# Column pairs for a short down projection, two scratch pools, an earlier norm chain, and three recurrent tiles projected ahead

## The chip, the core and the metric

The kernel runs on one core of a Trainium2 chip. The metric is device time in microseconds (us) of one execution. Engines are named as the profile names them: PE is TensorE's matmul (PEld its weight loads), ACT is ScalarE, DVE is VectorE, POOL is GpSimd, SP is SyncE, whose queue issues nearly all loads.

## The reference

Two residual layers over 256 tokens of width 2048. Layer 0 mixes tokens by attention, layer 1 by a gated linear recurrence; each is followed by a SwiGLU block of hidden width 5632. In short:

```python
for i in range(2):
    h = rms_norm(x, norm_mix[i])
    x = x + (attention_mixer(h, ...) if i == 0 else recurrent_mixer(h, ...))
    h = rms_norm(x, norm_ffn[i])
    x = x + (silu(h @ w_gate[i]) * (h @ w_up[i])) @ w_down[i]

# recurrent_mixer
xb, yb = split(h @ w_in, 2)
xb = depthwise_conv_width_4(xb) + bias
r, i = sigmoid(block_diag(xb, w_a) + b_a), sigmoid(block_diag(xb, w_i) + b_i)
log_a = -8 * r * softplus(-lam);  u = sqrt(1 - exp(2 * log_a)) * i * xb
h_t = exp(log_a_t) * h_(t-1) + u_t        # once forward, once backward in time
out = ((h_fwd + h_bwd) * gelu(yb)) @ w_out
```

Everything is in float32.

## The kernel before

**Products.** Each float32 operand is split into a rounded high part and a low rest (`hi`, `lo`), and a product is three matmuls: high by high, high by low, low by high. Weights arrive as halves of 8 blocks of 128x128 (512 KB, `load_half`, L110): a load on SP into `raw`, a cast on ACT to `hi` (L123), a subtraction on DVE to `lo` (L124), with five buffers of each. The list `order` (L163 to L171) fixes the sequence of all the halves.

**PE's order is written by hand**, instruction by instruction in program order. A counter, `step()`, advances once per triple of matmuls in the recurrence; `later(delay, fn)` hangs small work (the norm's broadcast, gates, scans) on a later step. The other engines' orders come from a planner that simulates the program; each engine then runs its list in order.

**FFN.** The hidden width is cut into parts of 12, 16 and 16 contraction tiles (`PARTS`). A part is made in units of four hidden tiles: gate and up projections as a pair of 512-wide columns (`unit`, `project_pair`), then `turned` (L458) transposes the product to feature-major (`tb`, then 16 copies into `tf`), and L795 and L796 split it into the operands `act`. Then the part is projected down and added to the residual `x_tok`. In a pair, two of the eight contraction steps (`SEVEN`, steps 2 and 5) use seven products in place of eight: `seven_forms` makes three sums of weights (`wx`, `wxh`, `wxl`, L264 to L272), `x_forms` the matching sums of operands, and `merge` (L333 to L337) puts the banks together. A step of a pair is two loads: 24 matmuls of 512 columns, or 21 with seven products. `down` does this for the 16-tile parts; the 12-tile part goes through `output` (L490), one column after another over all of its tiles, its matmuls at L247.

**Norm.** `Norm.add(c)` follows each finished column of the residual: squares with their sums, `turned`, then four operands `xg` (L418, L419). After the last column `finish()` makes the inverse root mean square, and for the recurrence's norm `spread()` makes diagonal matrices `ndg` (L444); 26 steps later two pairs of small matmuls (L450) turn them into a row vector per token, `nr.r` (`nrb`, L452).

**Recurrence.** It has 16 x tiles and 16 y tiles, in 8 blocks of two x and two y tiles. A tile is 16 contraction steps of three 256-wide matmuls (L341 to L343). Before block 0, `project_two` projects x tiles 0 and 1 over contraction tiles 0 to 11, then both over 12 to 15. The iteration of block b projects the x tiles of block b + 1 and the y tiles of block b, and has the gates, decays, scans and finishing of block b hung on the steps in `WHEN`. `conv_branch` (L822) multiplies a tile by `nr.r` into `cb`, convolves it in PSUM into `xc` and splits it into `xs`, the gates' operand. `load_gates` (L848) loads `graw`, casts it on ACT (`ghi`, L856) and subtracts on POOL (`glo`, L857).

**Scratch.** The FFN's scratch (`tb`, `tf`, `wx`, `fg`, `fu` and more) is one pool, `fp`. It is closed after layer 0, and the recurrence's pool `rp` is opened on the same memory; a tile there waits until what lay in its place was last read. PSUM has four banks for long sums (`acc`) and four for the rest (`pm`).

Of the kernel before, what the change touches and what calls it, by code (L numbers as in the profile page):

```python
# [31 lines left out]
LAST_STEPS = (0, 1, 3, 2, 4, 5, 6, 7)  # L32
# [4 lines left out]
COMMON = {"nsq", "nr", "nrt", "rsq_s", "nj", "ndg", "nrb"}  # L37
EPS = 1e-6
# [5 lines left out]
NORM = 26  # L44
# [7 lines left out]
WHEN = (18, 25, 32, 39, 42, 46, 50, 54, 58, 60, 62, 64, 66, 70, 74)  # L52
WHEN_LAST = (5, 9, 13, 17, 19, 20, 21, 24, 24, 25, 26, 27, 33, 39, 39)
# [20 lines left out]
def trunk(ctx, tc, w, out):  # L74
# [64 lines left out]
    def unit_steps(first):  # L139
        return FIRST_STEPS if first else USUAL_STEPS, True  # L140

    def down_steps(p, second):
        last = p == len(PARTS) - 1
        return LAST_STEPS if second and last else USUAL_STEPS, True

    def ffn_order(l):
        units = [wide(f"w_gate{l}"), wide(f"w_up{l}")]
        seq, i = [], 0
        for p, n in enumerate(PARTS):
            for _ in range(n // FOUR):  # L150
                for k, cols in pair_plan(*unit_steps(i == 0)):
# [105 lines left out]
    def seven_forms():  # L257
        load_half(*order[taken[0]])
        r1, w1 = flat(newest["raw"]), [flat(t) for t in newest["tiles"]]
        x, xh, xl = (fp[0].tile([P, 3, WIDE], t, tag=n, name=nm(n), bufs=1) for n, t in (("wx", F32), ("wxh", F32R), ("wxl", F32R)))  # L260
# [11 lines left out]
        dve.tensor_tensor(xl, x, xh[:].bitcast(F32), ALU.subtract)  # L272
        taken[0] += 2
        return [[t[:, k, :] for t in w] for w, k in ((w1, 0), (w1, 1), (w2, 0), (w2, 1), ((xh, xl), 0), ((xh, xl), 1), ((xh, xl), 2))]

    def x_forms(h0, h1, tag):
# [6 lines left out]
        t = fp[0].tile([P, 2, 4, P], F32R, tag=tag, name=nm(tag), bufs=1)  # L283
# [4 lines left out]
    def project_pair(xs, forms, order, middle, done):  # L288
        banks = [[new_acc() for _ in range(2)] for _ in range(2)]
        begun = set()  # L290

# [10 lines left out]
        steps = pair_plan(*order)  # L302
        seven = [n for n in order[0] if n in forms]
        for n, cols in steps:
            if n in forms:
# [6 lines left out]
                product(banks[0][0], tokens(2 * n + 1, 0), b21)  # L312
                product(banks[1][0], s4, b22)
# [3 lines left out]
                product(banks[0][1], tokens(2 * n + 1, 1), t4)  # L317
                if last:
                    middle(p1, q5, q6, q7)
            else:  # L320
                for j in cols:
                    half()
                    hi, lo = (flat(t) for t in newest["tiles"])
                    end = n == order[0][-1]
                    for a in range(2):
                        for k in range(2):
                            product(banks[j][a], tokens(2 * n + k, a), (hi[:, k, :], lo[:, k, :]), end and k == 1)
                    if end:
                        done(j, banks[j])

    def merge(p1, q5, q6, q7):
        g, u = (fp[0].tile([P, 2, WIDE], F32, tag=t, name=nm(t), bufs=1) for t in ("fg", "fu"))
# [72 lines left out]
    class Norm:  # L405
# [28 lines left out]
        def finish(self):  # L434
# [3 lines left out]
            self.rt = rsqrt(ms, "nr")  # L438


        def spread(self):
            dg = tmp("ndg", bufs=1)
            for a in range(2):
                dve.tensor_scalar(dg[:, a * P : (a + 1) * P], ident, self.rt[:, a : a + 1], None, ALU.mult)  # L444
# [8 lines left out]

            later(NORM, stage)

    def turned(src, both=True):  # L458
# [4 lines left out]
        for q in range(4):  # L463
            for i in range(4):
                o, y = f[32 * i : 32 * i + 32, q::4, :, :], b[32 * q : 32 * q + 32, :, i, :]
                y = y.rearrange("p a (k t) -> p a k t", k=FOUR)
                if i % 2 and both:
                    dve.tensor_copy(o, y)
                else:
                    act.copy(o, y)  # L470
# [4 lines left out]
    def open_ffn():  # L475
        fp[:] = [ffn_scope.enter_context(tc.tile_pool(name=nm("fp"), bufs=1))]
# [13 lines left out]
    def output(xs, norm=None, end=False, ready=0, close=None):  # L490
# [12 lines left out]
        if norm is not None:  # L503
            norm.finish()


    def down(xs, forms, p, norm=None, end=False):
        for c in (0, 2):
# [19 lines left out]
            project_pair(xs, forms, down_steps(p, c > 0), middle, done)  # L528
        if norm is not None:
            norm.finish()  # L530
# [244 lines left out]
    def ffn(norm, nxt):  # L775
        def unit(hid, forms, first):
# [12 lines left out]
            project_pair(norm.xs, norm.forms, unit_steps(first), lambda *banks: got.extend(merge(*banks)), done)  # L789
# [8 lines left out]
            for i, n in enumerate(SEVEN):  # L798
                if forms is not None and first <= 2 * n < len(hid):
                    forms[n] = x_forms(hid[2 * n], hid[2 * n + 1], f"hf{i}")  # L800

        for p, n in enumerate(PARTS):
            hid, forms = [], {} if n == KT else None
            for i in range(n // FOUR):
                unit(hid, forms, p == i == 0)
# [3 lines left out]
            if n == KT:  # L809
                down(hid, forms, p, nxt if last else None, last and nxt is None)  # L810
            else:
                output(hid)
# [4 lines left out]
    nr.spread()  # L817
# [3 lines left out]
    scope.append(rt.enter_context(tc.tile_pool(name="rp", bufs=2)))  # L821
# [99 lines left out]
    for b in range(-1, NBLK):  # L921
        blk, nxt = nxt, Block(b + 1) if b + 1 < NBLK else None
        if blk:
# [16 lines left out]
    def end_recurrence():  # L940
        rt.close()
        scope.pop()
# [91 lines left out]
```

## Time and profile before

| | |
|---|---|
| median of 3 runs | 2022.96 us (2022.78 to 2024.07) |
| the profiled execution's own time | 2022.37 us |
| its span, first to last instruction | 2020.6 us |
| PE busy | 1995.2 us, 99% of the span |
| DVE, ACT busy | 1666.0 us (82%), 1320.7 us (65%) |
| matmuls | 9944 |
| HBM read | 382.13 MB, 190 GB/s over the span |

Stages by the line of the matmuls, from the span's start: attention with its projections to 268 us (its output projection's columns from 184 on), layer 0's first part of the FFN to 395.6, its down projection to 467.5, the other two parts to 977.0, the recurrence to 1222.2, its output projection to 1309.5, layer 1's FFN to the end.

A profile row names line, engine, operation, the tile written and those read. "Busy" is the time in instructions; a matmul's end is modelled, so that matmuls overlap in the rows, and their starts tell the pace. "Granted clock" is the share of TensorE's full clock in a window. An idle time in brackets stands before an instruction, with the instruction that ended it.

### The profile page before, as it was taken

To read this page: it belongs to the slowest core of one execution; us is meant where nothing else is said; L and a number is where in the kernel's file an instruction comes from. 1 tells how busy PE (TensorE), PEld (TensorE's weight loads), DVE (VectorE), ACT (ScalarE), POOL (GpSimd) and SP (SyncE) were. 2 spreads that over 40 slices of the span, in tenths; PEclk is the share of its full clock that TensorE was granted. 3 is DMA by queue.
4 is the path that set the end of the run, shared out by engine and by line. 5 is a ranking of instruction groups with operands and counts; after the bars stand their busy time and mean duration, and the time that the engine had idled before them with its cause. 6 is when DMAs were issued, how large, how long until landed. Compare 5 with 4: busy or idle time off the path is not lost.

```text
span 2020.6 us, 27860 instructions
## 1 busy us (share of the span) xinstructions
PE 1995.2 (99%) x9944; PEld 1696.2 (84%) x9944; DVE 1666.0 (82%) x2347; ACT 1320.7 (65%) x2054; POOL 165.7 (8%) x213
## 2 busy tenths in 40 slices
PE   9999999999999999999899999999999999999999
PEld 8898888878888888887799998888788888888887
DVE  8998788856888888889868887898657898878897
ACT  7666666644667546677688898667545766457663
POOL 1463000000000000000133330000000000000000
PEclk9999999999999999999999999999999999999999
DMA  8444665656555665555555555655566566665564
GB/s 320 158 137 140 193 200 187 207 168 198 192 195 187 219 208 188 190 195 192 188 163 188 178 179 174 200 188 187 195 185 202 185 204 206 203 192 187 196 222 146
DMA packets 109004, 386.06 MB, mean 191 GB/s; under 512 B 12225, under 2 KB 12993, under 8 KB 108737
## 3 DMA queue, kind: packets, MB, share of 16 engines
q1 hardware_dynamic: 108720, 384.26, 58.0%
q8 instruction: 78, 1.28, 0.3%
q14 instruction: 62, 0.50, 0.1%
q10 hardware_dynamic: 144, 0.02, 0.0%
HBM read 382.13 MB, written 2.10 MB: 190 GB/s over the span
## 4 chain that ended last, share of the span: by engine, by line
PE 52%; issue 41%; DVE 4%; DMA 1%; ACT 1%; POOL 0%; DVEq 0%; SPq 0%; ACTq 0%; POOLq 0%
PE acc L294 24%; PE acc L247 7%; PE acc L225 6%; PE pm L294 4%; PE acc L341 3%; PE acc L342 3%; PE acc L343 3%; DVE lo L124 2%; PE pm L342 1%; PE pm L343 1%; PE pm L341 1%; DMA raw<-in_w_up_dram 1%; ACT hi L123 0%; DMA graw<-in_w_gates_dram 0%; ACT tf L470 0%
## 5 line engine op out<-in xcount | busy, mean ns | idle before, releaser
L123 ACT CAST hi<-raw 128x1024 fp32r<-128x1024 f32 (+1 forms) x708 | 730.4, 1045 | 486.1 <-PE acc L294 314.1
L124 DVE TENSOR_TENSOR lo<-raw,hi 128x1024 fp32r<-128x1024 f32 (+1 forms) x708 | 857.4, 1228 | 172.0 <-ACT hi L123 169.9
L294 PE MATMUL acc<-hi,xg 128*128 128x512 f32 x2200 | 694.4, 389 | 2.3 <-DVE fg L783 1.2
L294 PEld LDWEIGHTS acc<-hi,xg 128*128 128x128 f32 x2200 | 412.9, 188 | 91.0 <-DVE fg L783 2.0
L294 PE MATMUL acc<-lo,xg 128*128 128x512 f32 x1100 | 427.9, 389 | 0.0
L247 PE MATMUL acc<-hi,act 128*128 128x512 f32 x896 | 283.4, 395 | 6.2 <-ACT act L795 5.4
L294 PE MATMUL acc<-hi,act 128*128 128x512 f32 x800 | 252.7, 389 | 0.0
L294 PEld LDWEIGHTS acc<-lo,xg 128*128 128x128 f32 x1100 | 206.5, 188 | 42.4
L247 PEld LDWEIGHTS acc<-hi,act 128*128 128x128 f32 x896 | 170.7, 191 | 43.8 <-ACT act L795 6.3
L470 ACT COPY tf<-tb 32x256 f32<-32x256 f32 x448 | 180.8, 403 | 12.7 <-DVE tb L462 6.1
L294 PEld LDWEIGHTS acc<-hi,act 128*128 128x128 f32 x800 | 150.2, 188 | 32.3 <-issue 0.7
L247 PE MATMUL acc<-lo,act 128*128 128x512 f32 x448 | 176.8, 395 | 0.0
L294 PE MATMUL acc<-lo,act 128*128 128x512 f32 x400 | 155.6, 389 | 0.0
L342 PE MATMUL acc<-xg,hi 128*128 128x256 f32 x512 | 146.7, 286 | 2.0 <-DVE xg L419 1.9
L341 PE MATMUL acc<-xg,hi 128*128 128x256 f32 x512 | 146.8, 287 | 1.0 <-ACT xg L418 1.0
L343 PE MATMUL acc<-xg,lo 128*128 128x256 f32 x512 | 146.2, 285 | 0.0
L264 DVE TENSOR_TENSOR wx<-raw,raw 128x512 f32<-128x512 f32 x60 | 41.5, 692 | 123.7 <-DMA raw<-in_w_up_dram 97.1
L225 PE MATMUL acc<-xg,hi 128*128 128x512 f32 x384 | 127.1, 400 | 0.5 <-ACT hi L123 0.5
L271 ACT CAST wxh<-wx 128x1536 fp32r<-128x1536 f32 x60 | 88.9, 1482 | 49.6 <-DVE wx L267 46.7
L272 DVE TENSOR_TENSOR wxl<-wx,wxh 128x1536 fp32r<-128x1536 f32 x60 | 104.8, 1747 | 10.5 <-ACT wxh L271 10.5
L342 PEld LDWEIGHTS acc<-xg,hi 128*128 128x128 f32 x512 | 99.7, 195 | 2.5 <-DVE xg L419 2.4
L341 PEld LDWEIGHTS acc<-xg,hi 128*128 128x128 f32 x512 | 99.8, 195 | 1.5 <-ACT xg L418 1.3
(239 smaller groups left out, 2728.4 us busy)
## 6 DMA issues: line engine op xcount, KB each, us to landing
raw<-in_w_gate_dram SPq DMA_DIRECT2D x176, 512.0 KB, 4.0
raw<-in_w_up_dram SPq DMA_DIRECT2D x176, 512.0 KB, 4.4
raw<-in_w_down_dram SPq DMA_DIRECT2D x176, 512.0 KB, 4.2
raw<-in_w_in_dram SPq DMA_DIRECT2D x64, 512.0 KB, 4.6
raw<-in_w_qv_dram SPq DMA_DIRECT2D x40, 512.0 KB, 4.3
raw<-in_w_o_dram SPq DMA_DIRECT2D x32, 512.0 KB, 3.6
raw<-in_w_out_dram SPq DMA_DIRECT2D x32, 512.0 KB, 4.3
graw<-in_w_gates_dram SPq DMA_DIRECT2D x32, 256.0 KB, 3.6
```

The source lines that it names most:

```text
L123: newest["cast"] = act.copy(hi[:, sl, :], raw[:, sl, :])
L124: dve.tensor_tensor(lo[:, sl, :], raw[:, sl, :], hi[:, sl, :].bitcast(F32), ALU.subtract)
L225: pe.matmul(o, w, x, start=(k == 0 and not part), stop=(k == total - 1 and not part))
L247: pe.matmul(accs[a], x, wt[:, k, :], start=(k0 + k == 0 and n == 0), stop=(end and k == 1 and n == 2))
L264: dve.tensor_tensor(x[:, 0, :], r2[:, 0, :], r1[:, 0, :], ALU.add)
L271: act.copy(xh, x)
L272: dve.tensor_tensor(xl, x, xh[:].bitcast(F32), ALU.subtract)
L294: pe.matmul(acc, a, b, start=id(acc) not in begun, stop=last and i == 2)
L341: pe.matmul(o, hi, x[:, :S], start=start, stop=False)
L342: pe.matmul(o, hi, x[:, S:], start=False, stop=False)
L343: pe.matmul(o, lo, x[:, :S], start=False, stop=stop)
L470: act.copy(o, y)
```

## The change

- The 12-tile down projection goes through `down` and `project_pair`: the first 4 of its 6 contraction steps for both columns, then the last two for one column and for the other. It has no seven-product steps.
- In layer 0's last part, the second pair of columns (2 and 3) is projected as two columns, one after the other over all eight steps, with no seven-product steps. `LAST_STEPS` is gone; the second pair in layer 1's last part takes the usual order.
- `Norm.finish` is called inside `add` of the last column, after the squares and before `turned`. For the recurrence's norm it also runs `spread` there, and the turning copies of that column are ordered behind it: those on ACT behind the last table function, those on DVE behind the last `ndg`. `NORM` is 24.
- The FFN's scratch is two pools: `fq` with `tb` and `tf`, `fp` with the rest. The recurrence's is two on the same memory: `rq` with `cb`, `xc` and `gl`, `rp` with the rest.
- `project_ahead` projects x tiles 0, 1 and 2 over contraction tiles 0 to 11, then each over 12 to 15. Block 0's iteration projects one x tile and two y tiles (48 steps), with its work hung on `WHEN_FIRST`.
- `project_pair` takes a plan and takes its banks when they are first used.

```diff
-LAST_STEPS = (0, 1, 3, 2, 4, 5, 6, 7)
+SHORT = 6
+LOW = {"cb", "xc", "gl"}
-NORM = 26
+NORM = 24
+AHEAD = 3
 WHEN = (18, 25, 32, 39, 42, 46, 50, 54, 58, 60, 62, 64, 66, 70, 74)
+WHEN_FIRST = (20, 26, 32, 38, 40, 43, 46, 49, 51, 53, 55, 57, 59, 62, 66)
...
-        pl = tp if tag in COMMON else scope[-1]
+        pl = tp if tag in COMMON else scope[-2] if tag in LOW else scope[-1]
...
-    def pair_plan(steps, apart):
-        m = 1 + steps.index(SEVEN[-1]) if apart else len(steps)
-        return [(n, (0, 1)) for n in steps[:m]] + [(n, (j,)) for j in range(2) for n in steps[m:]]
+    def pair_plan(steps, together):
+        return [(n, (0, 1)) for n in steps[:together]] + [(n, (j,)) for j in range(2) for n in steps[together:]]
+    def unit_plan(first):
+        steps = FIRST_STEPS if first else USUAL_STEPS
+        return pair_plan(steps, 1 + steps.index(SEVEN[-1]))
+    def down_plan(n, alone):
+        if alone:
+            return pair_plan(range(n), 0)
+        return pair_plan(range(n), SHORT - 2 if n == SHORT else 1 + SEVEN[-1])
...
             down = wide(f"w_down{l}_{p}")
-            if n != KT:
-                seq += down
-                continue
             for c in range(0, len(down), n):
-                for k, cols in pair_plan(*down_steps(p, c > 0)):
+                for k, cols in down_plan(n // 2, l == 0 and p == len(PARTS) - 1 and c > 0):
                     seq += [down[c + n // 2 * j + k] for j in cols]
...
-        xin = range(2 * b + 2, 2 * b + 4) if b + 1 < NBLK else []
+        xin = range(AHEAD if b == 0 else 2 * b + 2, AHEAD if b < 0 else 2 * b + 4) if b + 1 < NBLK else []
...
-    def project_pair(xs, forms, order, middle, done):
-        banks = [[new_acc() for _ in range(2)] for _ in range(2)]
+    def project_pair(xs, forms, plan, middle, done):
+        banks = [[], []]
         begun = set()
+        def bank(j, a):
+            while len(banks[j]) <= a:
+                banks[j].append(new_acc())
+            return banks[j][a]
...
-    def project_two(xs, late):
-        banks = [new_acc() for _ in range(2)]
+    def project_ahead(xs, late):
+        banks = [new_acc() for _ in range(AHEAD)]
         for t in banks:
             sums(t[:, :S], half(), xs, 0)
-        rest = [half() for _ in range(2)]
+        rest = [half() for _ in banks]
...
         def add(self, c):
             for a in range(2):
                 act.activation(tmp("nj", (P, WIDE), bufs=1), x_tok[:, a, c, :], AF.Square, accum_out=self.sums[:, a, c : c + 1])
-            for f in turned(x_tok[:, :, c, :]):
+            behind = self.finish() if c == NCOL - 1 else None
+            for f in turned(x_tok[:, :, c, :], True, behind):
                 self.operand(f, True)
...
             self.rt = rsqrt(ms, "nr")
+            if not self.seven:
+                return prev[0], self.spread()
...
-                if i % 2 and both:
-                    dve.tensor_copy(o, y)
-                else:
-                    act.copy(o, y)
+                turn = dve.tensor_copy if i % 2 and both else act.copy
+                n = turn(o, y)
+                if behind is not None:
+                    follow(n, behind[i % 2])
...
-        fp[:] = [ffn_scope.enter_context(tc.tile_pool(name=nm("fp"), bufs=1))]
+        fp[:] = [ffn_scope.enter_context(tc.tile_pool(name=nm(s), bufs=1)) for s in ("fq", "fp")]
...
-            project_pair(xs, forms, down_steps(p, c > 0), middle, done)
-        if norm is not None:
-            norm.finish()
+            alone = norm is not None and c > 0
+            project_pair(xs, {} if alone else forms, down_plan(len(xs) // 2, alone), middle, done)
...
-            if n == KT:
-                down(hid, forms, p, nxt if last else None, last and nxt is None)
-            else:
-                output(hid)
+            down(hid, forms, nxt if last else None, last and nxt is None)
...
-    nr.spread()
...
-    scope.append(rt.enter_context(tc.tile_pool(name="rp", bufs=2)))
+    scope.extend([rt.enter_context(tc.tile_pool(name=s, bufs=2)) for s in ("rq", "rp")])
...
-            when = WHEN if nxt else WHEN_LAST
+            when = WHEN_FIRST if not blk.b else WHEN if nxt else WHEN_LAST
...
-            accs = (project_sum(nr.xs) for _ in range(2)) if blk else project_two(nr.xs, FOUR)
-            nxt.xcs = [conv_branch(2 * b + 2 + i, t) for i, t in enumerate(accs)]
-            if not blk:
+            if blk:
+                accs = (project_sum(nr.xs) for _ in range(2 - len(ahead)))
+                nxt.xcs = ahead + [conv_branch(2 * b + 2 + len(ahead) + i, t) for i, t in enumerate(accs)]
+                ahead = []
+            else:
+                xcs = [conv_branch(i, t) for i, t in enumerate(project_ahead(nr.xs, FOUR))]
+                nxt.xcs, ahead = xcs[:2], xcs[2:]
```

In `seven_forms`, `x_forms` and `merge` the scratch tiles that were taken from `fp[0]` are taken from `fp[1]`; `turned` and the first buffer of `x_forms` stay on `fp[0]`.

More of the change, by code (lines that the diff above doesn't have):

```diff
@@ L259, in seven_forms @@
         r1, w1 = flat(newest["raw"]), [flat(t) for t in newest["tiles"]]
-        x, xh, xl = (fp[0].tile([P, 3, WIDE], t, tag=n, name=nm(n), bufs=1) for n, t in (("wx", F32), ("wxh", F32R), ("wxl", F32R)))
+        x, xh, xl = (fp[1].tile([P, 3, WIDE], t, tag=n, name=nm(n), bufs=1) for n, t in (("wx", F32), ("wxh", F32R), ("wxl", F32R)))
         def sums(raw):
@@ L300, in tokens @@
             return [xs[k][:, o + a * P : o + (a + 1) * P] for o in (0, S)]
-        steps = pair_plan(*order)
-        seven = [n for n in order[0] if n in forms]
-        for n, cols in steps:
+        seven = [n for n, cols in plan if n in forms]
+        for n, cols in plan:
             if n in forms:
@@ L316, in project_pair @@
                 product(q6, s2, t2, last)
-                product(banks[0][1], tokens(2 * n + 1, 1), t4)
+                product(bank(0, 1), tokens(2 * n + 1, 1), t4)
                 if last:
                     middle(p1, q5, q6, q7)
-            else:
[L321 to L329, printed above, removed]
+                continue
+            end = n == plan[-1][0]
+            for j in cols:
+                half()
+                hi, lo = (flat(t) for t in newest["tiles"])
+                for a in range(2):
+                    for k in range(2):
+                        product(bank(j, a), tokens(2 * n + k, a), (hi[:, k, :], lo[:, k, :]), end and k == 1)
+                if end:
+                    done(j, banks[j])
     def merge(p1, q5, q6, q7):
-        g, u = (fp[0].tile([P, 2, WIDE], F32, tag=t, name=nm(t), bufs=1) for t in ("fg", "fu"))
+        g, u = (fp[1].tile([P, 2, WIDE], F32, tag=t, name=nm(t), bufs=1) for t in ("fg", "fu"))
         act.copy(g[:, 0, :], p1)
@@ L454, in spread, with turned @@
             later(NORM, stage)
-    def turned(src, both=True):
+            return i
+    def turned(src, both=True, behind=None):
         b = fp[0].tile([P, 2, FOUR, P], F32, tag="tb", name=nm("tb"))
@@ L502, in output, with down @@
                 norm.add(c)
-        if norm is not None:
-            norm.finish()
-    def down(xs, forms, p, norm=None, end=False):
+    def down(xs, forms, norm=None, end=False):
         for c in (0, 2):
@@ L775, in ffn, with unit @@
     def ffn(norm, nxt):
-        def unit(hid, forms, first):
+        def unit(hid, forms, parts, first):
             got = []
@@ L787, in done @@
                         dve.scalar_tensor_tensor(u[:, a, :], u[:, a, :], norm.rt[:, a : a + 1], g[:, a, :], ALU.mult, ALU.mult)
-            project_pair(norm.xs, norm.forms, unit_steps(first), lambda *banks: got.extend(merge(*banks)), done)
+            project_pair(norm.xs, norm.forms, unit_plan(first), lambda *banks: got.extend(merge(*banks)), done)
             u = got[1]
```

26 lines of the change are left out of this document (9 added, 17 removed).

## The prediction

> **What bounds the kernel now.** First the page's line of busy times, then busy times by stage, then TensorE's (PE's) instructions in order of time.
>
> ```profile
> span 2020.6 us, 27860 instructions
> PE 1995.2 (99%) x9944; PEld 1696.2 (84%) x9944; DVE 1666.0 (82%) x2347; ACT 1320.7 (65%) x2054; POOL 165.7 (8%) x213
> ```
>
> PE is never long without a matmul, so time comes back only where PE stands still, runs at a reduced clock, or gets fewer matmuls. A busy sum hides the second, since a matmul at half clock counts as busy; so I compare each stage's length with its matmul count at undisturbed pace. Columns: window and its length, then busy time (instructions) of PE, PEld, DVE, ACT, POOL, granted clock, DMA share, GB/s. The rows of 100.00 and 71.85 hold only the matmul line named (PE, PEld).
>
> ```profile
> 600.00:700.00 100.00, 100.00 (x442) 82.56 (x441) 1.00 0.61 200
> 1039.57:1068.23 28.66, 28.66 (x242) 28.66 (x241) 23.59 (x41) 25.28 (x44) 10.75 (x14) 1.00 0.55 181
> 395.59:467.53 71.94, 68.70 (x289) 55.82 (x288) 39.87 (x44) 33.63 (x45) 0.00 (x0) 0.95 0.55 172
> 1436.98:1508.83 71.85, 68.89 (x288) 55.73 (x287) 0.95 0.55 172
> 932.40:977.04 44.64, 42.45 (x187) 34.83 (x186) 43.90 (x67) 31.24 (x51) 0.00 (x0) 1.00 0.57 187
> 977.04:1222.24 245.20, 237.21 (x1926) 235.31 (x1924) 197.09 (x335) 209.99 (x365) 81.97 (x109) 0.97 0.55 172
> ```
>
> Counts include instructions that straddle an edge. The first row gives the pace of a 512-wide matmul: 100/441 = 0.2268 us. The second is one undisturbed recurrent block: 4 tiles x 16 contraction tiles x 3 + 4 gates x 12 = 240 matmuls 256 wide, 28.66/240 = 0.1194 us; a step (three of them) is 0.358 us. Against these paces:
>
> - Down projection of the 12-tile part, both layers: 4 x 6 loads x 12 = 288 matmuls, 65.3 us at pace; it took 71.94 and 71.85. Lost 6.6 + 6.5 = 13.1 us.
> - Last column pair before the recurrence: 6 x 24 + 2 x 21 = 186 matmuls, 42.2 us; it took 44.64. Lost 2.5 us.
> - Recurrence: 32 tiles x 48 + 32 gates x 12 = 1920 matmuls, 229.3 us, and 0.3 for the norm's four; it took 245.20. Lost 15.6 us.
>
> Together 31.2 us. The PE timeline shows where (start, duration, instruction, in brackets the idle time before it and what ended it):
>
> ```profile
> 409.34 0.51 PE L247 MATMUL acc<-hi,act 128*128 128x512 f32 x1 [2.71 <-ACT act L795]
> 410.82 1.22 PE L247 MATMUL acc<-hi,act 128*128 128x512 f32 x2 [0.54 <-DVE act L796]
> 1450.73 0.80 PE L247 MATMUL acc<-hi,act 128*128 128x512 f32 x1 [2.71 <-ACT act L795]
> 954.01 0.50 PE L294 MATMUL pm<-wxl,hf 128*128 128x512 f32 x1 [2.19 <-DVE wxl L272]
> 985.17 0.38 PE L342 MATMUL acc<-xg,hi 128*128 128x256 f32 x1 [1.91 <-DVE xg L419]
> 990.58 0.39 PE L341 MATMUL acc<-xg,hi 128*128 128x256 f32 x1 [0.99 <-ACT xg L418]
> 993.09 1.00 PE L450 MATMUL pm<-ndg,ones 128*128 128x128 f32 x4 [1.08 <-DVE ndg L444]
> 1005.62 0.35 PE L341 MATMUL pm<-xs,ghi 128*128 128x256 f32 x1 [1.69 <-ACT hi L123]
> 1008.58 0.58 PE L341 MATMUL pm<-xs,ghi 128*128 128x256 f32 x1 [1.82 <-DVE xs L378]
> ```
>
> The gaps explain half of it; the rest is the clock that falls after them:
>
> ```profile
> 406.25:416.60 10.35, 7.11 (x18) 4.83 (x17) 0.67 0.44 152
> 977.04:993.10 16.06, 11.94 (x80) 10.91 (x78) 15.20 (x38) 13.66 (x32) 0.20 (x4) 0.89 0.46 151
> 1005.60:1014.80 9.20, 6.99 (x33) 6.32 (x34) 7.67 (x14) 4.08 (x7) 1.56 (x5) 0.63 0.64 205
> ```
>
> The first holds 17 matmuls of 0.2268 us = 3.9 us in 10.35, clock 0.67: a wait of 2.71 us costs about twice itself.
>
> **The change part by part.**
>
> **(a) The 12-tile down projection goes in column pairs**, four contraction steps for both columns first. Before, column 0 alone met hidden tiles 8 to 11 after four loads, 4 x 2.72 = 10.9 us after 395.59, at 406.5. Now eight loads come first: 21.8 us, until 417.4. They are finished by:
>
> ```profile
> 408.89 1.32 ACT L795 CAST act<-tf 128x256 fp32r<-128x256 f32 x4
> 410.34 1.43 DVE L796 TENSOR_TENSOR act<-tf,act 128x256 fp32r<-128x256 f32 x4
> 398.56 1.05 ACT L123 CAST hi<-raw 128x1024 fp32r<-128x1024 f32 x1 [1.66 <-PE acc L247]
> 406.99 1.99 ACT L123 CAST hi<-raw 128x1024 fp32r<-128x1024 f32 x2
> 408.07 2.36 DVE L124 TENSOR_TENSOR lo<-raw,hi 128x1024 fp32r<-128x1024 f32 x2 [6.66 <-ACT hi L123]
> ```
>
> 411.8 against 417.4: 5.6 us to spare. The next to be late would be the weights. Weights have five buffers: the cast at 398.56, freed by the stage's first load, is that of the sixth; the seventh and eighth are the last two rows, done by 410.4, and PE reaches the seventh at 395.59 + 6 x 2.72 = 411.9. That is cover by 1.5 us. No forms are passed here, so the matmuls stay 288. Gain 13.1 us; bounds 6.5 (the wait stays in one layer) to 13.1.
>
> **(b) The last column pair of layer 0 becomes two whole columns without the seven-product steps.** Each of the two steps has 24 matmuls in place of 21: 6 x 0.2268 = **1.4 us added**. Gone are its sums, its merge and the 2.19 us wait for `wxl`. What may be late instead is the split of ordinary weights, since VectorE is full there:
>
> ```profile
> 932.40:954.70 22.30, 20.11 (x89) 16.36 (x88) 21.98 (x40) 18.30 (x34) 0.00 (x0) 1.00 0.55 174
> 954.70:977.00 22.30, 22.30 (x100) 18.46 (x99) 21.88 (x28) 12.90 (x17) 0.00 (x0) 1.00 0.59 200
> 978.17 2.38 DVE L468 COPY tf<-tb 32x256 f32<-32x256 f32 x8
> 987.54 2.38 DVE L468 COPY tf<-tb 32x256 f32<-32x256 f32 x8
> 984.64 1.66 DVE L419 SCALAR_TENSOR_TENSOR xg<-tf,pk,xg 128x256 fp32r<-128x256 f32 x4
> 990.56 1.69 DVE L419 SCALAR_TENSOR_TENSOR xg<-tf,pk,xg 128x256 fp32r<-128x256 f32 x4 [0.43 <-ACT xg L418]
> ```
>
> A column is 8 x 2.72 = 21.8 us. VectorE has in the third column 8 splits of 1.18 (the pair above) = 9.4 and what is left of two norm additions, about 11 (each 2.38 copies, 1.66 operands, about 2.6 of adds and transposes): 20.4, which fits; in the last column 9.4 + 6.6 = 16. I take no wait; bounds 0 to 2.2, by the old one. Net of the pair: 2.5 - 1.4 = 1.1 gained.
>
> **(c) The third column's operands come a column earlier**, so the 1.91 us wait at 985.17 (tiles 8 to 11) has 21.8 us of cover and goes. **(d) Three tiles run over twelve contraction tiles**: tiles 12 to 15 are wanted after 36 steps = 12.9 us from the recurrence's start, not 24 = 8.6. In before their last operation starts at 990.56, 13.5 us after 977.04, behind the third column's copies and operands (2.38 + 1.66 on VectorE, above). Without these it is 9.5. **The norm chain ahead of the turning copies** adds to that: it now stands between squares and copies, with the copies ordered behind it on both engines, and behind the waiting copies stand the casts of the next weights, for which PE waits in the end. Its steps in before:
>
> ```profile
> 989.96 0.17 DVE L437 TENSOR_SCALAR nrt<-nrt 128x2 f32<-128x2 f32 x1
> 991.63 0.19 ACT L541 ACTIVATE rsq_s<-nrt 128x2 f32<-128x2 f32 x1
> 992.75 0.48 DVE L444 TENSOR_SCALAR ndg<-ident,nr 128x128 f32<-128x128 f32 x2
> ```
>
> From the first Ln to the end of `ndg` 1.6 us, with sum and hand-overs 2 to 2.5. So the operands come at 11.5 to 12 of 12.9 us, about 1 us of cover; and `ndg` is ready near 5 us, before the norm's matmul at step 24 (8.6 us): the 1.08 goes. Bounds for (c) and (d): loss 0 to 6.4, what 78 matmuls (9.3 us) and the norm's 0.3 lack in the 16.06 us window above. The SyncE queue now carries the third tile's two halves ahead of block 0; five weight buffers still pace it, so I cost that at nothing.
>
> **(e) Two scratch pools.** Before, the gate weights' memory was still in use by the last operands, and SyncE held the load back; ScalarE then waited for it (landing 996.0), while the conv branch queued behind:
>
> ```profile
> SPq L855 <- DVE xg L419: 4.4, 1, 4.4
> 996.00 0.62 ACT L856 CAST ghi<-graw 128x512 fp32r<-128x512 f32 x1 [3.94 <-DMA graw<-in_w_gates_dram]
> 996.92 0.42 DVE L827 TENSOR_TENSOR cb<-acc,nrb 128x256 f32<-128x256 f32 x1 [3.69 <-ACT nrb L452]
> 1004.12 1.36 DVE L378 CAST xs<-xc 128x256 fp32r<-128x256 f32 x1
> 1008.24 0.29 DVE L378 CAST xs<-xc 128x256 fp32r<-128x256 f32 x1
> 1003.78 1.54 POOL L857 TENSOR_TENSOR glo<-graw,ghi 128x512 fp32r<-128x512 f32 x1 [0.59 <-ACT ghi L856]
> ```
>
> After, `tf` and `tb` lie under `cb`, `xc` and `gl` alone, so these loads can go early. The first gate needs both `xs`; they took from 996.92 to about 1009.2, 12.3 us with those stalls. Now tile 1 ends at step 44 and the gate stands at 48 + 20 = 68: 24 steps = 8.6 us, not 18 = 6.4, and the chain starts 4 steps earlier with tile 0: 10.0 us. Without ScalarE's waits I take the chain at about 8: no wait. Bounds: 0 to 5.3, what 33 matmuls (3.9 us) lack in the 9.20 us window above.
>
> **(f) Block 0's delays shrink** to 66 steps in 48 + 18. ScalarE has 25.28 us of work per block and now 48 x 0.358 + 4 x 1.43 = 22.9 us in this one; 2.4 us behind, made good in the next (28.66 - 25.28 = 3.4 spare). PE meets it only through weight casts, buffered five deep. **(g)** The other edits (the FFN norms' earlier chains, the last pair's step order in layer 1, banks taken at first use) touch no row with a wait: 0, bounds -1 to +1.
>
> **Sum.** 13.1 + 1.1 + 15.6 = 29.8 us. I leave 2 us for waits newly met in (d) to (f), between 0 and 11.7 (6.4 + 5.3), near the low end because each has cover. The profiled execution took 2022.37 us, span 2020.6; so 2022.4 - 27.8 = **1994.6 us**. The median of the runs is 2022.96, 0.6 above, which I leave in the range.
>
> **The rivals.** *VectorE late again at tiles 12 to 15* (chance 0.17). POOL's four `glo`, freed early, meet VectorE in (d): `xs` took 1.36 us beside one at 1003.78 and 0.29 alone. Four such meetings add 4 us to a chain with 1 us of cover; with the clock the 6.4 us of (d) stay. For: the cover is thin. Against: POOL can also run them before the last column ends. 1994.6 + 6.4 - 1 (of the 2 set aside) = 2000. The Trainium skill, SBUF — State Buffer, section "Who interferes with whom", says that VectorE and GpSimd share one port pair, which a VectorE instruction wants in a two-port mode or with two SBUF inputs, and that the loser waits. By that rule the weight splits (two inputs) would suffer as the copy did; the trace agrees for the copy, and which instructions will meet no row here shows.
>
> *The first gates wait as now* (0.12): 1994.6 + 5.3 = 1999.9, to 2001 with a further wait for PSUM. For it: block 0 has less room; against: 8 to 10 us for the chain.
>
> *The 12-tile part keeps its wait in one layer, its weights late* (0.05): cover there is 1.5 us; 1994.6 + 6.5 = 2001.
>
> *Slower* (0.05): the shortened block 0 leaves ScalarE behind for good, because its casts and gate functions queue in a fixed order, and gates of all seven further blocks wait as the first do now: 7 x 5.3 = 37 us on 1994.6, 2032. It decides from six waiting blocks (27.8/5.3 = 5.2). For: ScalarE at 25.28 of 28.66. Against: 3.4 us are made good per block.
>
> **How the numbers follow.** The forecast's case has 0.61. Its own range is 1991.5 (nothing newly met, and up to 1 us from (g)) to 1998. The range to 2001.5 takes in the next three cases' prices and leaves out the slower one and sums of two. A change of 0.2% (4 us) is about what a measurement of this kernel tells from none. All cases but the last are over 0.2% faster: 0.95. The last has 0.03 for six or more waiting blocks, slower by over 0.2%, and 0.02 for five (26.5 us of the 27.8 given back), within it.
>
> **What would show it.** In the profile of the changed kernel: no idle row ended by L795's successor in the 12-tile part and clock 1.00 there, 65 us for its 288 matmuls; 43.5 us for 192 matmuls in the last pair; the recurrence within 229.6 to 232 us, no idle row on operands or `ndg`; the gate loads issued before the last operands end. Wrong would be: a gap over 1.5 us in the first 13 us of the recurrence, a clock below 1.00 in its first 70 us, or blocks longer than 28.7 us.

## The result, and the profile after

| | before | changed |
|---|---|---|
| median | 2022.87 us (4 runs, 2021.08 to 2024.07) | 1996.62 us (4 runs, 1993.37 to 1997.10) |
| ratio, 95% interval | | 0.9868 (0.9850 to 0.9885) |
| profiled execution, its span | 2022.37, 2020.6 us | 1996.51, 1994.7 us |
| mean granted clock | 0.993 | 1.000 |

The change is faster by 26.2 us. The line numbers of the changed kernel differ a little (L300 is the pair's matmul, L346 to L348 are the recurrence's). Its page opens so:

```profile
span 1994.7 us, 27848 instructions
PE 1981.6 (99%) x9950; PEld 1686.1 (85%) x9950; DVE 1648.9 (83%) x2329; ACT 1317.0 (66%) x2051; POOL 167.6 (8%) x213
```

There are six matmuls more than before, and PE's share is still 99%, so this line hardly shows the 26 us. The stages do (columns as in the prediction: window and length, busy time of PE, PEld, DVE, ACT, POOL, granted clock, DMA share, GB/s): the 12-tile down projection of layer 0, the last column pair, the recurrence, layer 1's 12-tile down projection, and what follows it.

```profile
395.07:460.35 65.28, 65.28 (x290) 54.05 (x289) 38.49 (x43) 32.69 (x44) 0.00 (x0) 1.00 0.59 189
925.63:969.14 43.51, 43.51 (x193) 36.03 (x192) 38.47 (x61) 35.05 (x64) 6.03 (x4) 1.00 0.65 225
969.14:1200.84 231.70, 230.29 (x1925) 229.89 (x1924) 188.84 (x323) 204.97 (x351) 78.02 (x106) 1.00 0.55 174
1415.36:1480.64 65.28, 65.28 (x289) 54.07 (x288) 38.24 (x43) 32.68 (x44) 0.00 (x0) 1.00 0.59 186
1480.64:1990.80 510.16, 507.63 (x2233) 418.22 (x2231) 426.70 (x512) 305.94 (x404) 0.00 (x0) 1.00 0.58 194
```

PE is busy for the whole length of the first, second and fourth row, at a clock of 1.00: both down projections run at pace. Against before, 6.7 + 6.6 us came back there, 1.1 in the pair (six matmuls more included) and 13.5 in the recurrence: 27.9 us. The last row took 507.97 us in the kernel before; it is 2.2 us longer, which leaves 25.7 of the 25.9 us between the two profiled executions.

What PE still waited for (total, times, longest), from 185 us to 2000 us:

```profile
PE acc L300 <- DVE fu L792: 2.5, 3, 1.5
PE acc L300 <- DVE fg L789: 1.1, 2, 0.7
PE pm L346 <- DVE xs L383: 0.7, 1, 0.7
PE pm L347 <- DVE xs L384: 0.7, 1, 0.7
PE acc L300 <- DVE x_tok L529: 0.3, 1, 0.3
```

All waits on hidden tiles, on the norm's operands and on `ndg` are gone. Two of 0.7 us remain in front of the first gates; the rest are waits for banks in the FFNs.

### The profile page after: what moved, and what is told of

It reads as the page before. It is cut to its first block, busy times and chain, and to the rows that moved or that the text cites. A ratio compares the mean times of both kernels' runs of the same rounds, so it can differ in the third digit from the quotient of the medians.

```text
span 1994.7 us, 27848 instructions
## 1 busy us (share of the span) xinstructions
PE 1981.6 (99%) x9950; PEld 1686.1 (85%) x9950; DVE 1648.9 (83%) x2329; ACT 1317.0 (66%) x2051; POOL 167.6 (8%) x213
## 4 chain that ended last, share of the span: by engine, by line
PE 81%; DVE 11%; DMA 4%; issue 3%; ACT 1%; SPq 0%; POOL 0%; DVEq 0%; ACTq 0%
PE acc L300 49%; PE acc L248 8%; PE pm L300 6%; DVE lo L127 5%; PE acc L226 4%; PE acc L346 3%; PE acc L347 3%; PE acc L348 3%; DMA raw<-in_w_up_dram 2%; PE pm L348 1%; PE pm L347 1%; PE pm L346 1%; DMA raw<-in_w_down_dram 1%; ACT hi L126 1%; DVE raw L266 0%
## 5 line engine op out<-in xcount | busy, mean ns | idle before, releaser
L300 PE MATMUL acc<-hi,xg 128*128 128x512 f32 x2200 | 694.4, 389 | 2.9 <-DVE fu L792 1.8
L300 PEld LDWEIGHTS acc<-hi,xg 128*128 128x128 f32 x2200 | 412.9, 188 | 91.8 <-ACT wxh L272 3.7
L300 PE MATMUL acc<-lo,xg 128*128 128x512 f32 x1100 | 428.0, 389 | 0.0
L300 PE MATMUL acc<-hi,act 128*128 128x512 f32 x1212 | 379.4, 389 | 1.1 <-DVE fu L792 0.7
L300 PEld LDWEIGHTS acc<-hi,act 128*128 128x128 f32 x1212 | 227.5, 188 | 49.5 <-issue 1.8
L300 PEld LDWEIGHTS acc<-lo,xg 128*128 128x128 f32 x1100 | 206.5, 188 | 42.8
L300 PE MATMUL acc<-lo,act 128*128 128x512 f32 x606 | 235.7, 389 | 0.0
L477 ACT COPY tf<-tb 32x256 f32<-32x256 f32 x448 | 180.8, 403 | 10.3 <-DVE tb L471 3.9
L346 PE MATMUL acc<-xg,hi 128*128 128x256 f32 x512 | 144.8, 283 | 0.0
L347 PE MATMUL acc<-xg,hi 128*128 128x256 f32 x512 | 144.6, 282 | 0.0
L348 PE MATMUL acc<-xg,lo 128*128 128x256 f32 x512 | 144.4, 282 | 0.0
L300 PEld LDWEIGHTS acc<-lo,act 128*128 128x128 f32 x606 | 113.8, 188 | 23.5
L859 POOL TENSOR_TENSOR glo<-graw,ghi 128x512 fp32r<-128x512 f32 x32 | 49.5, 1545 | 777.5 <-ACT ghi L858 777.5
```

The costliest lines, as they stand in the source:

```text
L300: pe.matmul(acc, a, b, start=id(acc) not in begun, stop=last and i == 2)
L346: pe.matmul(o, hi, x[:, :S], start=start, stop=False)
L347: pe.matmul(o, hi, x[:, S:], start=False, stop=False)
L348: pe.matmul(o, lo, x[:, :S], start=False, stop=stop)
L477: n = turn(o, y)
L859: pool.tensor_tensor(lo, raw, hi[:].bitcast(F32), ALU.subtract)
```

## The experiments

| run | kernel | median us | ratio to before, 95% interval |
|---|---|---|---|
| e1 | before, with (a) alone | 2012.37 | 0.9942 (0.9928 to 0.9957) |
| e8 | before, with (a) and the two whole columns | 2003.74 | 0.9907 (0.9889 to 0.9925) |
| e2 | changed, one scratch pool each | 1999.99 | 0.9880 (0.9866 to 0.9895) |
| e3 | changed, two tiles ahead | 1995.37 | 0.9861 (0.9846 to 0.9876) |
| e4 | changed, last pair as before | 2010.54 | 0.9937 (0.9920 to 0.9954) |
| e5 | changed, norm chain last | 2002.32 | 0.9902 (0.9885 to 0.9920) |
| e7 | changed, again | 1996.04 | 0.9870 (0.9852 to 0.9887) |
| e6 | changed, first gates later | 1993.50 | 0.9861 (0.9840 to 0.9882) |
| e9 | two tiles ahead, first gates later | 1993.83 | 0.9857 (0.9844 to 0.9871) |
| e10 | e6 with six raw weight buffers | 1990.42 | 0.9837 (0.9824 to 0.9851) |

**e1, the down projection alone.** On the kernel before:

```diff
+        if PARTS[p] != KT:
+            return [(n, (0, 1)) for n in range(4)] + [(n, (j,)) for j in range(2) for n in (4, 5)]
...
-            if n == KT:
-                down(hid, forms, p, nxt if last else None, last and nxt is None)
-            else:
-                output(hid)
+            down(hid, forms, p, nxt if last else None, last and nxt is None)
```

> The kernel before, with the 12-tile down projection alone put into column pairs. Theory (each part gives back its own stage's loss): both waits on the last hidden tiles and the clock after them go, 13.1 us, so about 2009.8 us; the stage takes 65.3 us in each layer, the recurrence 245 us as before. Rival (the weights or the banks are late in the new order, or the gain of the whole change came from elsewhere): 2013 us or more, with a new idle row inside the stage.

Measured: 10.7 us faster (2023.09 to 2012.37), less than the theory's 13.1, and without the rival's idle row in the stage. Both stages took 65.28 us, as expected, and the recurrence stayed as it was. Of what is missing from 13.1 us, the largest piece lies in the last pair, which took 46.70 us (from 926.31) and not 44.64: its wait for `wxl` is a little longer than before, and here the clock falls after it (stages: layer 0's down projection, most of the last pair, the recurrence; then PE in order of time).

```profile
395.16:460.44 65.28, 65.28 (x289) 54.09 (x288) 39.15 (x44) 32.64 (x44) 0.00 (x0) 1.00 0.61 188
927.00:973.01 46.01, 43.67 (x184) 35.35 (x183) 44.17 (x67) 31.76 (x51) 0.00 (x0) 0.96 0.55 180
973.01:1217.83 244.82, 236.80 (x1925) 235.25 (x1924) 195.59 (x335) 210.49 (x364) 83.13 (x109) 0.97 0.55 172
```

```profile
948.37 0.66 PE L293 MATMUL pm<-wxl,hf 128*128 128x512 f32 x1 [2.30 <-DVE wxl L271]
948.83 1.05 PE L293 MATMUL pm<-wxh,hf 128*128 128x512 f32 x2
949.68 0.63 PE L293 MATMUL pm<-wxl,hf 128*128 128x512 f32 x1
950.11 0.63 PE L293 MATMUL pm<-wxh,hf 128*128 128x512 f32 x1
```

So (a) is worth its stage, and an old wait further on cost more than before by where it fell (the last section has the clock's rows for it).

**e8, the down projection and the two whole columns.** On e1:

```diff
+        if alone:
+            return [(n, (j,)) for j in range(2) for n in USUAL_STEPS]
+        return pair_plan(USUAL_STEPS, True)
...
+            alone = norm is not None and c > 0
+            project_pair(xs, {} if alone else forms, down_plan(p, alone), middle, done)
```

> The kernel before with the 12-tile down projection in pairs and the last pair of layer 0 as two whole columns, no more. Theory: against the first alone (2012.4 us) the pair gives its wait, the clock after it and the wait for tiles 8 to 11 less 1.4 us of matmuls; the late norm chain and the gate loads stay, 8 to 11 us lost in the recurrence: 2004 to 2008 us. Rival (the pair alone carries the rest): 2000 us or less.

Measured: 2003.74 us, 8.6 us below e1, just under the expected span. The recurrence lost 9.6 us, within the expected 8 to 11; the waits are the late norm chain and the first gates (waits of PE from 930 to 1040 us):

```profile
PE pm L340 <- DVE xs L377: 2.7, 2, 1.6
PE pm L449 <- DVE ndg L443: 2.2, 1, 2.2
PE pm L341 <- DVE xs L378: 0.3, 1, 0.3
```

No wait for operands is left, although only two tiles are ahead here: taking the third column's work out of the way was enough for that.

**e4, the last pair as before**, in the changed kernel:

```diff
-            return pair_plan(range(n), 0)
+            return pair_plan(LAST_STEPS, 1 + SEVEN[-1])
...
-            project_pair(xs, {} if alone else forms, down_plan(len(xs) // 2, alone), middle, done)
+            project_pair(xs, forms, down_plan(len(xs) // 2, alone), middle, done)
```

> The changed kernel with the last column pair of layer 0 as before (a pair, with seven-product steps). Theory: 6 matmuls fewer give 1.4 us, the wait for the weight sums costs 2.5 us again, and the last operands, behind the third column's again and with the norm chain ahead of them, come about 15 us after the recurrence's start where 12.9 are covered: 2 to 3 us of wait and up to 1.7 of clock; 2000 to 2003 us. Rival (36 steps cover this too): 1.4 us faster to 1 us slower than the changed kernel, 1995 to 1998 us.

Measured: 2010.54 us, 13.9 us above the changed kernel: far beyond theory and rival. The profiled execution was the fastest of the four, 2006.82 us, so that the profile shows 10.3 us of it: the pair took 1.2 us more (44.67 from 925.20 on, for 43.51), the recurrence 9.1 more (240.84 for 231.70). The wait is not where the theory put it. VectorE in order of time, and then the PE row:

```profile
974.65 0.69 DVE L530 TENSOR_TENSOR x_tok<-x_tok,acc 128x512 f32<-128x512 f32 x1
...
979.24 2.67 DVE L425 SCALAR_TENSOR_TENSOR xg<-tf,pk,xg 128x256 fp32r<-128x256 f32 x4
981.83 0.15 DVE L443 TENSOR_REDUCE nrt<-nsq 128x2 f32<-128x8 f32 x1
...
984.99 0.48 DVE L453 TENSOR_SCALAR ndg<-ident,nr 128x128 f32<-128x128 f32 x2
```

```profile
985.33 1.01 PE L459 MATMUL pm<-ndg,ones 128*128 128x128 f32 x3 [6.67 <-DVE ndg L453]
```

The recurrence starts at 969.87. The last column's residual is added only at 974.65, behind the third column's copies, and the third column's operands stand between it and the norm chain; `ndg` comes 15.5 us after the start, while PE has the norm's matmul at step 24 and waits 6.67 us there. Both columns' work in a row delays the chain and, behind it, the last operands, each by some 9 us against the changed kernel. The low parts of these operands start at 988.51, 18.6 us after the recurrence's start and not 15; PE had no wait for them only because it had already stood for `ndg`.

**e5, the norm chain last:**

```diff
-            behind = self.finish() if c == NCOL - 1 else None
-            for f in turned(x_tok[:, :, c, :], True, behind):
+            for f in turned(x_tok[:, :, c, :]):
                 self.operand(f, True)
+            if c == NCOL - 1:
+                self.finish()
```

> The changed kernel with the norm chain after the last column's operands, as before the change. Theory: the diagonal matrices come about 12 us after the recurrence's start, PE wants them at step 24, 8.6 us; a wait of 3 to 4 us and 1.7 to 3.4 us of clock: 2001 to 2004 us. Rival (the chain ahead costs the operands what it gives the norm): 1995.5 to 1998 us.

Measured: 2002.32 us, 5.7 us above the changed kernel, as the theory had it; the recurrence took 237.55 us. VectorE, then PE's wait:

```profile
978.87 1.67 DVE L424 SCALAR_TENSOR_TENSOR xg<-tf,pk,xg 128x256 fp32r<-128x256 f32 x4
983.31 0.48 DVE L453 TENSOR_SCALAR ndg<-ident,nr 128x128 f32<-128x128 f32 x2
```

```profile
PE pm L459 <- DVE ndg L453: 4.1, 1, 4.1
```

The low parts of the operands start at 978.87 here and at 978.98 in the changed kernel, against recurrence starts of 970.80 and 969.14: the chain ahead costs them 1.8 us, of which PE sees nothing, and spares 4.1 us of wait and the clock after it.

**e2, one scratch pool each:**

```diff
...
-        fp[:] = [ffn_scope.enter_context(tc.tile_pool(name=nm(s), bufs=1)) for s in ("fq", "fp")]
+        fp[:] = [ffn_scope.enter_context(tc.tile_pool(name=nm("fp"), bufs=1))] * 2
...
-    scope.extend([rt.enter_context(tc.tile_pool(name=s, bufs=2)) for s in ("rq", "rp")])
+    scope.extend([rt.enter_context(tc.tile_pool(name="rp", bufs=2))] * 2)
```

> The changed kernel with the scratch of the FFN and of the recurrence in one pool each. Theory: the gate loads wait again for the last operands, ScalarE waits for their landing in front of the conv branch, and the first gates lose 3 to 6 us more: 2000 to 2003 us. Rival (the first gates wait for the conv branch's 12 us on VectorE, whatever the loads do): within 1 us of the changed kernel, 1995.6 to 1997.6 us.

Measured: 1999.99 us, at the edge of the theory's span and 3.4 above the changed kernel by the medians (the intervals of the ratios overlap). The recurrence took 236.44 us, 4.7 more, with 3.9 us of waits in front of the first gates and the next tile, where the changed kernel has 1.4, and a stretch at half clock behind them (granted clock 0.50 from 998.78 to 1002.19). ScalarE, VectorE and POOL:

```profile
983.83 0.62 ACT L858 CAST ghi<-graw 128x512 fp32r<-128x512 f32 x1 [4.04 <-DMA graw<-in_w_gates_dram]
986.52 0.56 ACT L831 ACTIVATE acc<-cb,pk 128x256 f32<-128x256 f32 x1
```

```profile
988.81 1.21 DVE L127 TENSOR_TENSOR lo<-raw,hi 128x1024 fp32r<-128x1024 f32 x1
990.33 1.92 DVE L127 TENSOR_TENSOR lo<-raw,hi 128x1024 fp32r<-128x1024 f32 x1
```

```profile
989.60 1.58 POOL L859 TENSOR_TENSOR glo<-graw,ghi 128x512 fp32r<-128x512 f32 x1 [2.51 <-ACT ghi L858]
991.66 1.72 POOL L859 TENSOR_TENSOR glo<-graw,ghi 128x512 fp32r<-128x512 f32 x1 [0.49 <-ACT ghi L858]
```

ScalarE stands 4.04 us for the gate weights with the conv branch behind it, as in the kernel before; and a weight split beside `glo` takes 1.92 us where one alone takes 1.21. How the 4.7 us divide between the two isn't shown. With two pools the four `glo` ran from 924.7 us on, under the FFN:

```profile
924.69 1.30 POOL L859 TENSOR_TENSOR glo<-graw,ghi 128x512 fp32r<-128x512 f32 x1 [740.39 <-ACT ghi L858]
...
935.82 1.60 POOL L859 TENSOR_TENSOR glo<-graw,ghi 128x512 fp32r<-128x512 f32 x1 [1.43 <-ACT ghi L858]
```

**e3, two tiles ahead:**

```diff
-AHEAD = 3
+AHEAD = 2
...
-            when = WHEN_FIRST if not blk.b else WHEN if nxt else WHEN_LAST
+            when = WHEN if nxt else WHEN_LAST
```

> The changed kernel with two tiles ahead, not three, and the usual delays in block 0. Theory (cover counts): tiles 12 to 15 are wanted 8.6 us after the recurrence's start and come at about 10.2, and the first gates stand 18 steps behind tile 1 with a conv branch of 12 us; about 1.6 + 4 us of waits and 2 to 4 us of clock: 2002 to 2006 us. Rival (the earlier third column, the earlier norm chain and the two pools carry the gain, the third tile nothing): below 1999 us.

Measured: 1995.37 us, no slower than with three. The theory fell. In the profile the recurrence took 233.51 us, 1.8 more than with three tiles, and layer 1's FFN happened to be shorter by more. PE's waits there:

```profile
PE pm L346 <- DVE xs L383: 0.8, 1, 0.8
PE pm L347 <- DVE xs L384: 0.7, 2, 0.4
PE acc L347 <- DVE xg L424: 0.7, 1, 0.7
```

ScalarE made the operands' high parts from 978.32 on, 8.75 us after the start at 969.57. PE took the first of them at 978.88, right behind the norm's matmuls, without a wait; the first low part came 0.7 us late. And the first gates waited hardly longer (1.6 us in all, not 1.4) with 18 steps between tile 1 and them than with 24: with two tiles, less stands in the conv branch's way, 10.3 us from the first row at 981.71 to `xs` complete at 992.06, against 12.1 with three.

**e7, the changed kernel again.** No edit.

> The changed kernel again. The 1.5 us wait at 1569.5 us in layer 1's FFN: if it follows from the order of instructions, it is there again, and the FFN of layer 1 takes 702.9 us; if it follows from when loads happen to land, it is elsewhere or gone, and that stage takes 700 to 704 us. Time 1995.5 to 1997.5 us.

Measured: 1996.04 us. The recurrence took 231.70 us again, with the same waits of 0.7 us. The 1.5 us wait at 1569.5 is gone; others, of up to 1.1 us, stand at 674, 1654 and 1697 us (waits of PE from 185 to 2000 us):

```profile
PE acc L300 <- DVE x_tok L529: 1.6, 2, 1.0
PE acc L300 <- DVE fu L792: 1.3, 2, 1.1
```

So the waits at the transition came back unchanged, as those of a program would, and those in the FFNs moved from one execution to the other.

**e6, the first gates later:**

```diff
-WHEN_FIRST = (20, 26, 32, 38, 40, 43, 46, 49, 51, 53, 55, 57, 59, 62, 66)
+WHEN_FIRST = (25, 30, 35, 40, 41, 43, 46, 49, 51, 53, 55, 57, 59, 62, 66)
```

> The changed kernel with the first block's gates on steps 25, 30, 35, 40 (20, 26, 32, 38) and its first decay on 41 (40). Theory: five more steps, 1.8 us, cover the conv branch; the two idle times of 0.7 us in front of the first gates go with what follows them: 1994 to 1996 us, the recurrence about 230.2 us long. Rival (the block's end is pushed onto the next block's gates): as the changed kernel or slower, 1996.5 us or more.

Measured: 1993.50 us, 3.1 below the changed kernel by the medians; the intervals overlap. The recurrence is what tells: 229.89 us, PE busy for all of it, no wait left.

```profile
969.13:1199.02 229.89, 229.89 (x1925) 229.81 (x1924) 187.97 (x323) 204.08 (x350) 77.92 (x105) 1.00 0.56 175
```

**e9, two tiles ahead and later gates.** The changed kernel with

```diff
-AHEAD = 3
+AHEAD = 2
...
-WHEN_FIRST = (20, 26, 32, 38, 40, 43, 46, 49, 51, 53, 55, 57, 59, 62, 66)
+WHEN_FIRST = (23, 29, 35, 41, 44, 47, 50, 54, 58, 60, 62, 64, 66, 70, 74)
```

> The changed kernel with two tiles ahead and the first block's gates on steps 23, 29, 35, 41 of a block of 64 steps. Theory (in the kernel as changed the third tile buys only steps in front of the first gates): those 0.8 and 0.7 us waits go, the 0.7 us wait for the last operands stays, the recurrence takes 230.5 to 231.5 us: 1993.5 to 1996 us, as with three tiles and later gates. Rival (the third tile's cover carries part of the gain): a recurrence of 233 us or more, 1996.5 us or more.

Measured: 1993.83 us, the recurrence 231.69 us, with the 0.7 us for the last operands still there and 0.3 left in front of the gates. The rival's mark, 233 us, was not reached, though the stage is 0.2 us above what the theory had. Two tiles and first gates two to five steps later than `WHEN`'s do what three tiles do in the changed kernel; with gates late enough, the third tile is worth 1.8 us of the stage (231.69 against 229.89), which the times don't resolve.

**e10, six raw buffers.** e6 with

```diff
-        raw = wp.tile([P, HALF, P], F32, tag="raw", name=nm("raw"), bufs=5)
+        raw = wp.tile([P, HALF, P], F32, tag="raw", name=nm("raw"), bufs=6)
```

> The kernel with later gates (three tiles) with six buffers for raw weights in place of five. Theory: the idle times of 0.3 to 1.5 us in the two FFNs come from loads that land late, and a load issued one buffer earlier takes 1 to 2 us of them: FFN stages of 700.5 and 700.8 us, 1992 to 1993.5 us. Rival (the banks wait for VectorE's own order): the same idle times, 1993 to 1996 us.

Measured: 1990.42 us, the fastest of all and below both expected spans, 32.9 us under the kernel before as measured beside it (2023.36). Against e6, from which it differs by the one buffer, it is 3.1 us lower by the medians, but the intervals overlap (0.9824 to 0.9851, 0.9840 to 0.9882). Four of its five executions took 1990.03 to 1990.57 us. The fifth, 1994.68 us, is the profiled one, and its rows can't explain the other four; there PE waited 4.7 us from 185 us on (2.5 us for `fg` in the first units of the two layers, 1.4 in the recurrence), where it waited 3.5 in e6's profile. Whether the sixth buffer is worth anything, and whether by the loads' lead, is not shown.

## Why the prediction was right

The forecast was 1994.6 us in a range of 1991.5 to 2001.5; the median is 1996.62.

**(a)** 13.1 us for both layers. Shown: 65.28 us for 288 matmuls in each, as at pace, and in e1 with this part alone. The weights' cover of 1.5 us held.

**(b)** 43.5 us for 192 matmuls. Shown: 43.51, VectorE busy 38.47 of it and never late. The term counted 1.1 us; undoing the edit costs 13.9 by the medians (e4). That isn't a contradiction of the sum, which put most of it under (c) and (d), but the text named the operands of tiles 8 to 11 as what the earlier third column frees. The larger thing is the norm chain: behind the third column's work `ndg` came 15.5 us after the start (e4), without it 6.2.

**(c), (d)** The waits for operands and `ndg` went, as forecast. The cover was mis-sized: I took the operands at 11.5 to 12 us of 12.9. They started at 978.98, 9.8 us after 969.14, so that 8.6 us of two tiles would nearly have been enough, and e3 showed it: 0.7 us of wait. I charged the chain's 2 to 2.5 us in full; it took 1.8. What was more off is the 9.5 us without the chain: e5 has 8.1 there (978.87 less 970.80). The last column's residual is now added from 968.86 on, before the recurrence starts, where the kernel before added its last half at 980.58, 3.5 us after the start. So the third tile, which the prediction costed as 4.3 us of needed cover, carries at most 1.8 us. VectorE's rows of the last column, from its last addition to the last operand:

```profile
968.86 1.28 DVE L529 TENSOR_TENSOR x_tok<-x_tok,acc 128x512 f32<-128x512 f32 x2
...
974.90 0.48 DVE L452 TENSOR_SCALAR ndg<-ident,nr 128x128 f32<-128x128 f32 x2
975.41 2.39 DVE L477 COPY tf<-tb 32x256 f32<-32x256 f32 x8
...
978.98 1.67 DVE L424 SCALAR_TENSOR_TENSOR xg<-tf,pk,xg 128x256 fp32r<-128x256 f32 x4
```

**(e)** The gate loads went early, as forecast, and without that 4.7 us of the recurrence come back (e2). The chain of the conv branch was mis-sized: 8 us forecast. From tile 0's first row to tile 1's last it took 12.1, as before, though no gate load stood in it:

```profile
984.24 0.43 DVE L829 TENSOR_TENSOR cb<-acc,nrb 128x256 f32<-128x256 f32 x1 [2.44 <-PE acc L348]
...
995.89 0.42 DVE L384 TENSOR_TENSOR xs<-xc,xs 128x256 fp32r<-128x256 f32 x1
```

Between them stand five weight splits of 1.22 us and a third tile's operations. The cover was 10.0 us; the rest is the two waits of 0.7 us and what PE loses around them: the 2.1 us by which the stage exceeds 229.6. They took up the 2 us set aside for waits newly met. That the sum held is luck here: the reserve was meant to be small because each wait had cover, and at the first gates the cover was missing. Five more steps in front of them give it (e6).

**(f)** Shown: no wait on ScalarE. A window of 28.70 us behind block 0 holds a block's 240 matmuls and three that reach over its edges, as an undisturbed block before does in 28.66 with two. ScalarE is busy for 27.14 us of it, not 25.28, as it makes good what it was behind.

```profile
1021.90:1050.60 28.70, 28.70 (x243) 28.70 (x242) 25.08 (x46) 27.14 (x48) 10.34 (x16) 1.00 0.57 177
```

**(g)** Nothing plus or minus 1 us was wrong for the profiled execution: the FFN of layer 1 behind its first part took 2.2 us more, by waits for banks. That the change makes them is not shown: the repeat has them elsewhere, and in the runs on the changed kernel, with the same order on PE there, the stage took anything from 506.9 (e10) to 510.2 us (e4), 507.97 before. The same program's times spread over some 3.7 us (1993.37 to 1997.10). In the profiled execution, 1996.51 us, these waits are the 2 us above the forecast; the median has no profile of its own.

**The rivals.** POOL did not meet the norm chain: its four `glo` were over by 937.5 us. The first gates did wait, by the mechanism of that rival but for 1.4 us and not 5.3. The 12-tile part kept no wait. ScalarE recovered after block 0 (e6, no wait in any block).

## What to carry to other kernels

Where one engine is busy for 99%, measure each stage against its instruction count at undisturbed pace: length less count times pace found 31.2 us here, of which 27.9 came back, while the idle rows alone gave half of it. It says what a stage has lost, not what a change will cover: both covers of the recurrence were mis-sized. At a change of stage, find the short serial chain (here a norm's scale) that queues behind bulk work of the same engine, and put it first; then see whether the bulk still needs more cover, since an added cover may turn out to be spare. Memory shared between two stages is also an order: put the scratch that is used last under the tiles that are needed last.

## What the runs showed of the hardware that was not expected

Waits of nearly one size had different prices. In the profile before, the 2.19 us wait for `wxl` at 954.01 was followed by the full clock (the window 954.70 to 977.00 has 1.00); in e1 one of 2.30 us at the same place was followed by a stretch at half clock (0.96 over 46.01 us, matmuls started 0.43 us apart, not 0.23), and in the profile before 1.91 us of wait at 985.17 was, too.

The granted clock shows what sets them apart. In the profile before, the stretches at half clock are 409.69 to 416.52, 986.54 to 989.96, 993.37 to 996.78, 1007.02 to 1013.85 and 1450.76 to 1457.58 us. Each is 3.41 or 6.83 us long, and all their edges lie on one grid of 3.41 us, wherever the waits are. Cut along this grid, with the wait at 954.01, then that at 985.17 in the kernel before, and e1's wait at 948.37 (columns as above):

```profile
952.41:955.82 3.41, 1.80 (x8) 1.50 (x9) 3.38 (x4) 0.00 (x0) 0.00 (x0) 1.00 0.60 216
955.82:959.23 3.41, 3.41 (x17) 2.83 (x16) 3.34 (x5) 2.73 (x3) 0.00 (x0) 1.00 0.07 20
983.13:986.54 3.41, 1.50 (x11) 1.37 (x11) 3.41 (x8) 2.64 (x7) 0.00 (x0) 1.00 0.54 166
986.54:989.96 3.42, 3.04 (x15) 2.75 (x14) 3.26 (x10) 3.02 (x8) 0.00 (x0) 0.50 0.68 224
```

```profile
945.14:948.56 3.42, 1.12 (x6) 0.62 (x5) 3.42 (x6) 1.05 (x2) 0.00 (x0) 1.00 0.97 344
948.56:951.97 3.41, 3.41 (x9) 2.64 (x9) 3.31 (x5) 1.11 (x2) 0.00 (x0) 0.50 0.09 36
```

The 2.19 us wait began before 952.41, so that 1.61 us of it fell into the first window; 1.91 and 2.30 us fell whole into theirs. In the twelve profiles, from 185 to 1980 us, all thirteen windows at full clock in which PE stood still for 1.8 us or more in all (the least 1.83, by two waits of about 1 us) were followed by one at half clock, and none with 1.61 us or less was. So part of what a wait costs is chance, by where it falls. In the changed kernel the windows with the most idle time have 1.4 and 1.5 us, not far below.

The Trainium skill, TensorE: Matmul & The Clock Gate, section "Why this matters for your kernels", advises no idle gaps over some 3 us between bursts; here gaps of 1.9 to 2.7 us lowered the clock in some cases and not in others, and the measurement decides. The same page, "What's actually happening", says that the monitor's windows of 3.4 us run freely; the trace agrees, with stretches on one grid of 3.41 us that begin at no fixed distance from a wait.
